# First tile stored in three column pieces, tiles 3 to 6 loaded by one DMA (contrast adjustment, 1 core)

## The chip, the core and the metric

The kernel runs on one core of one Trainium2 chip. The metric is device time in microseconds. Five runs of the kernel before gave a median of 239.35 us (239.29 to 239.66).

## What is computed

The input is a batch of 16 images with 3 channels of 512 x 512 float32 pixels. Every one of the 48 planes is moved away from its own mean and clipped:

```python
def reference(x, factor):                       # x: 16 x 3 x 512 x 512 float32, factor 1.5
    mean = np.mean(x, axis=(2, 3), keepdims=True)
    return np.clip(mean + factor * (x - mean), 0, 1).astype(np.float32)
```

The kernel computes it as `factor * x + (1 - factor) * mean`, followed by a max with 0 and a min with 1. Input and output have 50.33 MB each, and each byte crosses once.

## The kernel before

The 48 planes are cut into 12 tiles of 4 planes. A tile is 128 partitions of 8192 float32 (32 KB a partition, 4 MiB in all); 32 partitions hold one plane. `ring` is one tensor with six slots of a tile each (`BUFS = 6`); tile t lives in slot `t % 6`, is loaded there, changed in place and stored from there. Below, tiles are numbered from 0, so "tiles 3 to 6" of the title are tiles 2 to 5 in the code.

Each tile passes through `compute(t)`, in this order:

- VectorE sums columns 0 to 4351 of each partition (`tensor_reduce`, L89), and at the same time ScalarE sums the other 3840 columns by an activation with an accumulator (L92).
- TensorE multiplies both partial sums by the constant block matrix `blockw` (L94 and L95). The result, `bias[:, t]`, holds for each partition the shift of its plane.
- VectorE makes two passes over the whole tile: multiply and add (L96), then max and min (L99).
- `store` (L112) issues the tile's output DMAs from ScalarE's queue.

The order is written out by hand (`tc.manual_schedule`), and each engine works through its own list in this order. SyncE's queue issues all loads (L84): tile 0 in two parts (2048 and 6144 columns), then tiles 1 to 5, one DMA each. After `compute(t)`, the load of tile t + 6 follows; it waits until all stores of tile t have landed, since it overwrites that slot. ScalarE issues all stores, so the sum of tile t + 1 on ScalarE stands behind the stores of tile t.

The stores of tile 0 are special. `RAMP` lists eight DMAs; each takes every 4th partition from a first partition q, so 32 partitions, and a range of columns. The contiguous stretches that they write grow from 4 KB to 32 KB. All eight stand after the two whole-tile passes L96 and L99. Tiles 1 to 11 leave in one DMA each, with 128 stretches of 32 KB.

Each DMA signals its end on one of eight shared counters, so an issue can also wait for the end of an earlier DMA that had the same counter. In the program before, the sixth, seventh and eighth store of tile 0 wait in this way on ScalarE's queue, and the loads of tiles 3, 4 and 5 on SyncE's queue.

Of the kernel before, what the change touches and what calls it, by code (L numbers as in the profile page):

```python
# [1 line left out]

# [4 lines left out]


P = 128  # L10
ROW = 8192
BUFS = 6
SHORT = 2048

RAMP = [
    (0, 4, 0, 1024),
    (1, 4, 0, 2048),
    (0, 4, 1024, 4096),
    (2, 4, 0, 4096),
    (2, 4, 4096, ROW),  # L20
    (0, 4, 4096, ROW),
    (1, 4, 2048, ROW),
    (3, 4, 0, ROW),
]
SUM = 4352


@with_exitstack
def kernel(
    ctx: ExitStack,  # L30
    tc: tile.TileContext,
    x: bass.AP,
    factor: float,
    out: bass.AP,
):

    nc = tc.nc
    f32 = mybir.dt.float32  # L40
    Alu = mybir.AluOpType
    Act = mybir.ActivationFunctionType

    B, C, H, W = x.shape
    n_img, n_pix = B * C, H * W
    ppi = n_pix // ROW
    per_tile = P // ppi
    n_tiles = n_img // per_tile
    assert ppi * ROW == n_pix and per_tile * n_tiles == n_img

    factor = float(factor)
    wconst = (1.0 - factor) / float(n_pix)

    x_f = x.rearrange("b c h w -> (b c h w)")
    out_f = out.rearrange("b c h w -> (b c h w)")


    consts = ctx.enter_context(tc.tile_pool(name="consts", bufs=1))
    xpool = ctx.enter_context(tc.tile_pool(name="xpool", bufs=1))
    small = ctx.enter_context(tc.tile_pool(name="small", bufs=1))  # L60
    psum = ctx.enter_context(tc.tile_pool(name="psum", bufs=1, space=bass.MemoryType.PSUM))


    sums = small.tile([P, 2 * n_tiles], f32, name="sums")
    junk = small.tile([P, ROW - SUM], f32, name="junk")
    bias = psum.tile([P, n_tiles], f32, name="bias")

    blockw = consts.tile([P, P], f32, name="blockw")
    nc.gpsimd.memset(blockw, 0.0)  # L69
    for a in range(0, P, ppi):  # L70
        nc.gpsimd.memset(blockw[a : a + ppi, a : a + ppi], wconst)  # L71


    ring = xpool.tile([P, BUFS, ROW], f32, name="ring")

    def load(t, c0=0, c1=ROW, n=1):

        b = t % BUFS
        src = bass.AP(
            tensor=x_f.tensor,  # L80
            offset=t * P * ROW + c0,
            ap=[[ROW, P], [P * ROW, n], [1, c1 - c0]],
        )
        nc.sync.dma_start(out=ring[:, b : b + n, c0:c1], in_=src)  # L84

    def compute(t):
        xt = ring[:, t % BUFS, :]
        own = sums[:, 2 * t : 2 * t + 2]
        nc.vector.tensor_reduce(  # L89
            out=own[:, 0:1], in_=xt[:, 0:SUM], axis=mybir.AxisListType.X, op=Alu.add  # L90
        )
        nc.scalar.activation(out=junk, in_=xt[:, SUM:ROW], func=Act.Copy, accum_out=own[:, 1:2])  # L92
        shift = bias[:, t : t + 1]
        nc.tensor.matmul(shift, blockw, own[:, 1:2], start=True, stop=False)  # L94
        nc.tensor.matmul(shift, blockw, own[:, 0:1], start=False, stop=True)  # L95
        nc.vector.tensor_scalar(  # L96
            out=xt, in0=xt, scalar1=factor, scalar2=shift, op0=Alu.mult, op1=Alu.add
        )
        nc.vector.tensor_scalar(  # L99
            out=xt, in0=xt, scalar1=0.0, scalar2=1.0, op0=Alu.max, op1=Alu.min  # L100
        )
        for piece in RAMP if t == 0 else [(0, 1, 0, ROW)]:
            store(t, *piece)

    def store(t, q=0, parts=1, c0=0, c1=ROW):

        dst = bass.AP(
            tensor=out_f.tensor,
            offset=(t * P + q) * ROW + c0,
            ap=[[parts * ROW, P // parts], [1, c1 - c0]],  # L110
        )
        nc.scalar.dma_start(out=dst, in_=ring[q::parts, t % BUFS, c0:c1])  # L112

    with tc.manual_schedule():
        load(0, c1=SHORT)
        load(0, c0=SHORT)
        load(1)
        for t in range(2, BUFS):
            load(t)
        for t in range(n_tiles):  # L120
            compute(t)
            if t + BUFS < n_tiles:
                load(t + BUFS)


# [1 line left out]
_INS = ['x', 'factor']  # L127
_OUTS = [((16, 3, 512, 512), 'float32')]

_NUMBERS = {'factor': 1.5}  # L130


# [26 lines left out]
```

## Time and profile before

The profiled execution took 239.3 us, with a span of 237.5 us between its first and last instruction; the other 1.8 us lie outside of it. The clock granted to TensorE was 1.0 throughout.

| row of the profile | value |
|---|---|
| time of the profiled execution / its span | 239.3 us / 237.5 us |
| data moved | 100.67 MB, mean 424 GB/s over the span |
| VectorE busy | 162.4 us (68% of the span) |
| L89, L96, L99: one instruction on VectorE | 4.680, 4.491, 4.427 us |
| ScalarE busy | 43.2 us (18%) |
| L92: one instruction on ScalarE | 3.403 us |
| load queue (q1): packets, share of the 16 DMA engines | 1872, 49.7% |
| store queue (q10): packets, share of the 16 DMA engines | 1968, 49.1% |

The page gives for each engine the time in which it executed something. For transfers it gives what the 16 DMA engines moved, and how long the packets of each queue occupied them. A packet here is one contiguous stretch in a partition, or one 4-byte signal at the end of a DMA on one DMA engine. The page's 40 slices cut the span into equal parts of 5.94 us, and each digit is a busy share in tenths.

### The profile page before, as it was taken

The numbers are of one execution on the slowest core, as the hardware profiler recorded it, in microseconds if no ns is written. First come the engines' busy times: TensorE is split into PE (matmuls) and PEld (weight loads), VectorE is DVE, ScalarE is ACT, GpSimd is POOL, SyncE is SP. The second block draws the span as 40 slices with busy tenths as digits, with TensorE's granted clock in tenths as the row PEclk, the third lists the DMA queues.
The fourth block names the chain that finished last, engine by engine and source line by source line (L and its number), as shares of the span: only waits on it lengthen the run. The fifth ranks groups of instructions, "written<-read, shape, count | busy, mean of one in ns | idle before, by whom it ended". The sixth has DMA issues, their size and how long they took to land.

```text
span 237.5 us, 298 instructions
## 1 busy us (share of the span) xinstructions
PE 13.9 (6%) x48; PEld 11.9 (5%) x48; DVE 162.4 (68%) x36; ACT 43.2 (18%) x25; POOL 0.9 (0%) x9
## 2 busy tenths in 40 slices
PE   0010000010100101010010100101000001000000
PEld 0010000010100101010010100101000001000000
DVE  0079930059899898999989899898998658900000
ACT  2050000320505014050320505014050040000000
POOL 1000000000000000000000000000000000000000
DMA  7999999999999999999999999999999999999996
GB/s 292 414 441 441 441 410 421 367 469 430 430 414 419 436 441 441 441 441 436 441 425 430 403 425 441 441 441 441 441 436 436 425 419 415 430 441 441 441 441 265
DMA packets 3841, 100.67 MB, mean 424 GB/s; under 512 B 512, under 2 KB 512, under 8 KB 544
## 3 DMA queue, kind: packets, MB, share of 16 engines
q1 hardware_dynamic: 1872, 50.33, 49.7%
q10 hardware_dynamic: 1968, 50.33, 49.1%
q14 instruction: 1, 0.01, 0.0%
HBM read 50.33 MB, written 50.33 MB: 424 GB/s over the span
## 4 chain that ended last, share of the span: by engine, by line
DMA 42%; DVE 28%; another core or an unknown queue 8%; issue 5%; PE 2%; ACTq 1%; SPq 0%; ACT 0%; DVEq 0%
DMA out_dram<-ring 26%; DMA ring<-in_x_dram 16%; DVE ring L96 11%; DVE ring L99 11%; DVE sums L89 6%; PE bias L95 1%; ACTq L112 1%; PE bias L94 1%; SPq L84 0%; ACT junk L92 0%; DVEq L96 0%; ACTq L92 0%; DVEq L89 0%
## 5 line engine op out<-in xcount | busy, mean ns | idle before, releaser
L96 DVE TENSOR_SCALAR ring<-ring,bias 128x8192 f32<-128x8192 f32 x12 | 53.9, 4491 | 26.4 <-PE bias L95 23.4
L92 ACT ACTIVATE junk<-ring 128x3840 f32<-128x3840 f32 x12 | 40.8, 3403 | 152.5 <-DVE ring L99 86.2
L89 DVE TENSOR_REDUCE sums<-ring 128x1 f32<-128x4352 f32 x12 | 56.2, 4680 | 18.1 <-DMA ring<-in_x_dram 18.1
L99 DVE TENSOR_SCALAR ring<-ring 128x8192 f32<-128x8192 f32 x12 | 53.1, 4427 | 0.4
L94 PE MATMUL bias<-sums,blockw 128*128 128x1 f32 x24 | 7.0, 361 | 182.4 <-ACT junk L92 182.4
L94 PEld LDWEIGHTS bias<-sums,blockw 128*128 128x128 f32 x24 | 6.0, 311 | 183.3 <-ACT junk L92 167.0
L95 PE MATMUL bias<-sums,blockw 128*128 128x1 f32 x24 | 7.0, 362 | 2.0 <-DVE sums L89 1.5
L95 PEld LDWEIGHTS bias<-sums,blockw 128*128 128x128 f32 x24 | 6.1, 313 | 2.9 <-DVE sums L89 2.2
L92 ACT ACTIVATION_READ_ACCUMULATOR junk<-ring 128x1 f32 x12 | 2.2, 186 | 0.0
L92 ACT ACT_TABLE_LOAD x1 | 1.3, 1283 | 0.7 <-PEq L140 0.7
L71 POOL MEMSET blockw<- 32x32 f32 x4 | 0.5, 116 | 0.2
L69 POOL MEMSET blockw<- 128x128 f32 x1 | 0.2, 204 | 0.3 <-POOLq L140 0.3
L140 POOL MEMSET const-bfloat16-1.0<- 128x1 bf16 x1 | 0.1, 111 | 0.0
L140 POOL MEMSET const-uint8-127<- 128x1 uint8 x1 | 0.1, 111 | 0.0
L140 POOL MEMSET const-float32-1.0<- 128x1 f32 x1 | 0.1, 108 | 0.0
L140 POOL MEMSET const-float32-0.0<- 128x1 f32 x1 | 0.1, 103 | 0.2 <-issue 0.2
## 6 DMA issues: line engine op xcount, KB each, us to landing
ring<-in_x_dram SPq DMA_DIRECT2D x11, 4096.0 KB, 26.5
out_dram<-ring ACTq DMA_DIRECT2D x11, 4096.0 KB, 44.0
ring<-in_x_dram SPq DMA_DIRECT2D x1, 3072.0 KB, 11.6
out_dram<-ring ACTq DMA_DIRECT2D x3, 512.0 KB, 24.5
ring<-in_x_dram SPq DMA_DIRECT2D x1, 1024.0 KB, 4.7
out_dram<-ring ACTq DMA_DIRECT2D x1, 1024.0 KB, 24.6
out_dram<-ring ACTq DMA_DIRECT2D x1, 768.0 KB, 27.4
out_dram<-ring ACTq DMA_DIRECT2D x1, 384.0 KB, 16.3
```

Of the source, the lines that this page charges most:

```text
L69: nc.gpsimd.memset(blockw, 0.0)
L71: nc.gpsimd.memset(blockw[a : a + ppi, a : a + ppi], wconst)
L89: nc.vector.tensor_reduce(out=own[:, 0:1], in_=xt[:, 0:SUM], axis=mybir.AxisListType.X, op=Alu.add)
L92: nc.scalar.activation(out=junk, in_=xt[:, SUM:ROW], func=Act.Copy, accum_out=own[:, 1:2])
L94: nc.tensor.matmul(shift, blockw, own[:, 1:2], start=True, stop=False)
L95: nc.tensor.matmul(shift, blockw, own[:, 0:1], start=False, stop=True)
L96: nc.vector.tensor_scalar(out=xt, in0=xt, scalar1=factor, scalar2=shift, op0=Alu.mult, op1=Alu.add)
L99: nc.vector.tensor_scalar(out=xt, in0=xt, scalar1=0.0, scalar2=1.0, op0=Alu.max, op1=Alu.min)
L112: nc.scalar.dma_start(out=dst, in_=ring[q::parts, t % BUFS, c0:c1])
L140: nc = _bacc.Bacc("TRN2", target_bir_lowering=False, num_devices=1)
```

## The change

The first tile's two passes are cut by columns into three pieces of 2048, 3072 and 3072 columns (8, 12 and 12 KB a partition). Each piece is passed over twice and stored at once, by a DMA over all 128 partitions. The list `RAMP` goes. The four loads of tiles 2 to 5 become one DMA of 128 x 4 x 8192 elements, of 16 MiB; within a partition its four stretches of 32 KB come from four tiles, which lie 4 MiB apart in the input. All other loads, stores and sums stay as they are.

```diff
-RAMP = [
-    (0, 4, 0, 1024),
-    (1, 4, 0, 2048),
-    (0, 4, 1024, 4096),
-    (2, 4, 0, 4096),
-    (2, 4, 4096, ROW),
-    (0, 4, 4096, ROW),
-    (1, 4, 2048, ROW),
-    (3, 4, 0, ROW),
-]
+FIRST = (SHORT, 3072, 3072)
...
-        nc.vector.tensor_scalar(
-            out=xt, in0=xt, scalar1=factor, scalar2=shift, op0=Alu.mult, op1=Alu.add
-        )
-        nc.vector.tensor_scalar(
-            out=xt, in0=xt, scalar1=0.0, scalar2=1.0, op0=Alu.max, op1=Alu.min
-        )
-        for piece in RAMP if t == 0 else [(0, 1, 0, ROW)]:
-            store(t, *piece)
+        c = 0
+        for n in FIRST if t == 0 else [ROW]:
+            part = xt[:, c : c + n]
+            nc.vector.tensor_scalar(
+                out=part, in0=part, scalar1=factor, scalar2=shift, op0=Alu.mult, op1=Alu.add
+            )
+            nc.vector.tensor_scalar(
+                out=part, in0=part, scalar1=0.0, scalar2=1.0, op0=Alu.max, op1=Alu.min
+            )
+            store(t, c, c + n)
+            c += n
 
-    def store(t, q=0, parts=1, c0=0, c1=ROW):
-
-        dst = bass.AP(
-            tensor=out_f.tensor,
-            offset=(t * P + q) * ROW + c0,
-            ap=[[parts * ROW, P // parts], [1, c1 - c0]],
-        )
-        nc.scalar.dma_start(out=dst, in_=ring[q::parts, t % BUFS, c0:c1])
+    def store(t, c0, c1):
+        nc.scalar.dma_start(out=dram(out_f, t, c0, c1), in_=ring[:, t % BUFS, c0:c1])
 
     with tc.manual_schedule():
         load(0, c1=SHORT)
         load(0, c0=SHORT)
         load(1)
-        for t in range(2, BUFS):
-            load(t)
+        load(2, n=BUFS - 2)
```

`dram(ap, t, c0, c1)` is a new helper that names columns c0 to c1 of tile t in the input or output. The loop over the tiles is unchanged.

More of the change, by code (lines that the diff above doesn't have):

```diff
@@ L55, with dram @@
     out_f = out.rearrange("b c h w -> (b c h w)")
+    def dram(ap, t, c0=0, c1=ROW):
+        return bass.AP(tensor=ap.tensor, offset=t * P * ROW + c0, ap=[[ROW, P], [1, c1 - c0]])
     consts = ctx.enter_context(tc.tile_pool(name="consts", bufs=1))
```

## The prediction

> **What bounds the kernel now.** I read the page's 40 slices first, then the DMA queues, then the busy times by stretch, then the chain of waits around the first store, then the timeline of ScalarE's and SyncE's queues.
>
> ```profile
> DVE  0079930059899898999989899898998658900000
> DMA  7999999999999999999999999999999999999996
> ```
>
> VectorE has holes, at 30 to 48 us and at the end. The DMA row has none: 9 from the second slice to the last but one.
>
> ```profile
> q1 hardware_dynamic: 1872, 50.33, 49.7%
> q10 hardware_dynamic: 1968, 50.33, 49.1%
> ```
>
> Loads and stores together occupy the 16 DMA engines for 98.8% of the span. The bytes are fixed, so the span is data over rate, plus the start, plus the end, plus whatever is moved below the usual rate. The busy times by stretch show where that is (the last two columns are the DMA share and GB/s):
>
> ```profile
> 4.00:28.00 24.00, 1.14 (x4) 1.00 (x4) 14.37 (x4) 3.50 (x2) 0.00 (x0) 1.00 1.03 442
> 28.00:32.00 4.00, 0.00 (x0) 0.00 (x0) 3.83 (x1) 0.00 (x0) 0.00 (x0) 1.00 1.05 452
> 32.00:36.00 4.00, 0.00 (x0) 0.00 (x0) 0.00 (x0) 0.00 (x0) 0.00 (x0) 1.00 0.89 372
> 36.00:40.00 4.00, 0.00 (x0) 0.00 (x0) 0.00 (x0) 0.00 (x0) 0.00 (x0) 1.00 1.03 426
> 40.00:44.00 4.00, 0.00 (x0) 0.00 (x0) 0.00 (x0) 0.00 (x0) 0.00 (x0) 1.00 0.96 344
> 44.00:48.00 4.00, 0.00 (x0) 0.00 (x0) 0.00 (x0) 2.63 (x1) 0.00 (x0) 1.00 1.02 438
> 48.00:192.00 144.00, 11.57 (x40) 9.95 (x40) 130.62 (x29) 32.33 (x20) 0.00 (x0) 1.00 1.00 433
> ```
>
> The steady rate is 433 GB/s; 100.66 MB at it are 232.5 us, so 5.0 us of the span are start, end and slow stretches. From 28 to 48 us the mean is 406 GB/s: 20 us x (1 - 406/433) = 1.2 us lost. With 4 to 28 us, which shares packets over the window's edge, it is 44 us x (1 - 426/433) = 0.7 us. The packet records lie between: a 32 KB read takes 1.213 us everywhere else, and some 50 reads from 32.9 to 43.7 us take 1.25 to 2.0 us; their excess, over 16 engines, is 0.9 us. They follow the first three pieces of tile 0 (4, 8 and 12 KB), mostly right behind a piece's 4-byte end signals (33, 37.5 and 42.3 us). Behind the 16 to 32 KB pieces none is stretched.
>
> How the two queues share the engines is in the queue rows of 31 to 44 us and of 72 to 192 us:
>
> ```profile
> q1 hardware_dynamic: 148, 4.26, 83.2%
> q10 hardware_dynamic: 145, 0.84, 15.4%
> ...
> q10 hardware_dynamic: 899, 26.31, 50.8%
> q1 hardware_dynamic: 881, 25.59, 49.4%
> ```
>
> Packets go one for one, whatever their size: with short store packets the loads get most of the time, with equal packets half. The chain shows what held tile 1:
>
> ```profile
> 28.49 16.33 DMA out_dram<-ring
> 44.83 0.02 issue
> 44.85 0.48 ACTq L112
> 45.32 0.05 issue
> 45.37 0.07 ACT junk L92
> ```
>
> ScalarE sat until 44.85 us before its eighth store issue, so the sum of tile 1 began at 45.37, and store 1 was issued at 59.02. Nothing of that stopped the DMA row.
>
> **The change, part by part.**
>
> *Packets.* For tile 0's stores each engine gets 24 packets (8 of 8 KB, 16 of 12 KB) in place of 16. By the records a packet takes 0.159, 0.309, 0.460, 0.611, 1.213 us for 4, 8, 12, 16, 32 KB: 0.008 us beside the bytes. So +8 x 0.008 = +0.07 us. DMAs fall from 32 to 24, each with one end signal of 0.009 us an engine: -0.07 us. Sum 0.
>
> *VectorE in tile 0.* L96 and L99 (4.49 + 4.43 us) become six instructions. No row has these widths; proportional they cost the same 8.92 us, and the nearest row for an instruction's fixed part is POOL's 0.10 to 0.20 us, so 4 x 0.2 = +0.8 us at most that I expect, hidden as the DMA engines read on. The first piece is done at 18.28 + 2.2 to 2.6 = about 20.8 us (now 27.25), the last at about 28.1.
>
> *ScalarE.* Three issues instead of eight; none waits for a transfer that is still running. The sum of tile 1 starts behind the third, at 28.5 instead of 45.4 us, and by the rows of tile 0 (3.6 + 1.2 + 8.95 us) store 1 is issued near 42.4 instead of 59.0.
>
> *The one load.* It removes three issues of 0.33 us on SyncE and two waits there (29.3 us for a load to land); SyncE bounds nothing. But tiles 2 to 5 now land together, and VectorE waits. When? Loads 0 and 1 are in by 2.2 + 8.39 MB/433 = 21.6 us. Now the first store packets come after 30 us (the queue rows of 27 to 30 us have none) for an issue at 27.27; with the same 4 us, the pieces flow from about 25 us. Until then the load passes 2.8 of its 32 packets an engine. Then 24 rounds, 24 x 1.213 + 8 x 0.309 + 16 x 0.460 = 39.0 us, to 64.0; then 5.2 rounds against store 1, 5.2 x 2.43 = 12.6, to 76.6. It lands near 77 us; bounds are 2.2 + 25.2 MB/433 = 60.3 (no store passes) and 2.2 + 33.6 MB/433 = 79.7 (both stores first).
>
> *What is late next.* Tile 2 starts on VectorE at 77 instead of 58.9. A tile takes 14.3 us there (start to start in the timeline of tiles 2 and 3), so tile 2 is ready at 91.4, tile 3 at 105.7, tile 11 at 77 + 143 = 220 (now 207.3). Do the DMA engines run dry? Before store 3, they have loads 0 to 7 and stores 0 to 2: 11 x 4.194 = 46.1 MB, until 2.2 + 106.5 = 108.7 us. Store 3's data flows at 105.7 + 0.4 issue + 1.0 (0.74 to 1.75 us, the first load's packets) = 107.1: 1.6 us to spare. Before store 2: 41.9 MB, until 99.1 against 92.8. Before store 4: 13 tiles, until 128 against 121.4. Before store 11: 96.5 MB, until 225 against 221.4. The tightest place has cover, so the late tiles cost 0. If the load lands at its upper bound, store 3 flows at about 110.2 and the gap is 1.5 us; cover ends at a landing past 78.6. Load 6 waits for three ends instead of eight; store 0 ends by about 65 to 70 (load 6 now starts at 69.6), behind the large load in the queue anyway: 0.
>
> *The stretched reads.* What becomes of the 0.9 us is open. Lower bound 0: -0.9. Upper bound, by rounds: six rounds of 4 to 12 KB lost 0.9, 0.15 each, so 24 would lose 3.6: +2.7. I take the row it is nearest to: the excess sits at three end signals of short pieces, and the new kernel has three. So 0.9 again, net 0.
>
> *A rule against it.* In the stretch from 48 to 192 us, where an engine's successive reads are neighbouring rows of 32 KB, the rate is 433 GB/s; no row here has reads 4 MiB apart. The Trainium skill (DMA: Bandwidth & Descriptors, Latency and other measured facts) reports that a partition pitch of 4 MiB halves a copy's rate, from 207 to 103 GB/s a direction. [...]
>
> Sum on the profiled execution: 239.3 + 0.07 - 0.07 + 0 = 239.3; the median is 239.35, the same within the runs. A difference below 0.2% (0.48 us) can't be told from none here.
>
> **Rivals.**
>
> *Faster: the stretch goes.* If it belongs to the 32-partition pieces or the 4 KB start, the reads keep 1.213 us: 239.35 - 0.9 = 238.45. For: pieces from 16 KB up stretch nothing. Against: two of the three new pieces have the 12 KB of the worst stretched moment. 0.28.
>
> *Slower: every short round stretches.* All 24 rounds with 8 and 12 KB packets lose 0.15 us: 239.35 + 2.7 = 242.05. It decides from (0.9 + 0.48)/24 = 0.06 us a round. For: the lowest rate, 344 GB/s, is with 12 KB pieces. Against: the excess lies at few moments, not at every round. 0.18.
>
> *Slower: the DMA engines run dry near 108 us.* Landing past 78.6 us opens a gap of up to 1.5 us: up to 240.9. Against: the one-for-one sharing puts it at 77. 0.12.
>
> *Not what it says:* the load split again, or the ring not free. The built program has one 128 x 4 x 8192 transfer; this is in the forecast's rest.
>
> **How the numbers follow.** Forecast "same" 0.42, at 239.3. Faster 0.28, slower 0.18 + 0.12 = 0.30. The range goes from below the faster case (238.3) past the gap case (240.9) to 241.2; it leaves out the 24-round case, 0.18.
>
> **What would show it.** DMA row without a hole; the first store issue near 21 us, store 1 near 42; VectorE idle from about 42 to 77, then without pause for ten tiles; the last load landed near 190; store 11 issued near 220. A DMA share well below 1 around 97 to 110 us would show the gap; a rate below 420 GB/s through 25 to 65 us the stretched rounds; 433 through 25 to 65 the faster case. I am wrong if the last store is issued after 225 us or the large load lands past 80.

## The result and the profile after

| | kernel before | kernel after |
|---|---|---|
| median time | 239.32 us (46 runs, 239.04 to 240.42) | 239.96 us (27 runs, 239.38 to 241.23) |
| median span | 237.5 us (237.3 to 237.8) | 238.0 us (237.4 to 239.1) |
| median time outside of the span | 1.79 us (1.74 to 1.85) | 2.06 us (1.78 to 2.18) |

The span and the outside time of the kernel before come from 69 further runs of it, timed beside the experiments.

The change made the kernel slower by 0.64 us: the ratio is 1.0027, with an interval of 1.002 to 1.0033. About 0.5 us of the loss lies inside the span and 0.25 to 0.3 us outside of it; medians do not add up exactly. The forecast was "same" at 239.3 us. The time lies inside the range, but 0.27% is more than the 0.2% that counted as no change. The profiled execution of after took 239.85 us, with a span of 237.7 us, so its trace holds only about 0.2 us of the 0.5 us.

The 40 slices of after, VectorE and the DMA engines:

```profile
DVE  0079989000001899898989989899898989989000
DMA  7999999999999999999999999999999999999996
```

VectorE's hole is longer and starts later than before (41.6 to 71.3 us in whole slices), and VectorE works until later: three idle slices at the end, where before had five. The DMA row has no hole, as before. The two queues (packets, MB, share of the 16 DMA engines) and the one large load (KB, then us from issue to landing):

```profile
q1 hardware_dynamic: 1824, 50.33, 49.6%
q10 hardware_dynamic: 2016, 50.33, 49.1%
...
ring<-in_x_dram SPq DMA_DIRECT2D x1, 16384.0 KB, 74.2
```

It landed 74.2 us after its issue at 2.1 us, so at about 76.3 us, where 77 was predicted. The waits of VectorE for a load (total us, number of waits, longest) and ScalarE's timeline (start, duration, engine, line, operation, count) give the rest of the schedule:

```profile
DVE sums L81 <- DMA ring<-in_x_dram: 47.1, 2, 34.3
```

```profile
20.75 7.39 ACTq L101 DMA_DIRECT2D out_dram<-ring  x3
...
42.10 0.34 ACTq L101 DMA_DIRECT2D out_dram<-ring  x1
76.42 3.40 ACT L84 ACTIVATE junk<-ring 128x3840 f32<-128x3840 f32 x1 [44.68 <-DMA ring<-in_x_dram]
...
90.78 0.34 ACTq L101 DMA_DIRECT2D out_dram<-ring  x1
...
105.08 0.34 ACTq L101 DMA_DIRECT2D out_dram<-ring  x1
```

The first piece leaves at 20.75 us, store 1 is issued at 42.10 us, and then VectorE waits for 34.3 us. Tile 2 starts at 76.4 us, store 2 is issued at 90.78 us, store 3 at 105.08 us, store 11 at 219.4 us. The prediction had 20.8, 42.4, 77, 91.4, 105.7 and 220. So the schedule is the predicted one within 0.7 us. What was not foreseen stands in the busy times by stretch (the last two columns are the DMA share and GB/s):

```profile
24.00:64.00 40.00, 1.17 (x4) 1.00 (x4) 17.25 (x6) 3.50 (x2) 0.00 (x0) 1.00 1.00 426
64.00:88.00 24.00, 1.17 (x4) 1.00 (x4) 10.85 (x3) 3.50 (x2) 0.00 (x0) 1.00 1.01 437
92.00:96.00 4.00, 1.18 (x4) 1.00 (x4) 3.35 (x1) 2.67 (x2) 0.00 (x0) 1.00 0.93 393
```

From 92 to 96 us the rate is 393 GB/s; the kernel before had 434 GB/s in that stretch. The DMA queues between 88.5 and 93.5 us show what surrounds it, first in after, then in before:

```profile
q1 hardware_dynamic: 80, 2.10, 98.0%
```

```profile
q10 hardware_dynamic: 35, 1.15, 53.1%
q1 hardware_dynamic: 33, 0.98, 45.5%
```

After has no row for q10 there: nothing is stored. Store 1's last data packet ends at 85.8 us and its last end signal at 87 us; store 2 is issued at 90.78 us, and its first packet comes 4.2 us later, at 94.95 us. Reads alone keep the engines at 98.0%, so no hole shows in the DMA row. In the packet records six reads from 90.7 to 94.1 us, on five of the 16 DMA engines, take 0.15 to 0.47 us longer than the 1.213 us of a 32 KB packet.

Sorted by engine, the packet records of these two executions also give the end of each of the 16. The mean end of the transfers is even earlier than before, 235.78 against 235.98 us. The slowest engine, with which the span ends, finishes at 236.53 us against 236.33 us. It lags the mean by 0.75 us, and 0.64 us of its time are the two reads of these six that fell to it.

### The profile page after: what moved, and what is told of

The parts are those of the page before. It is cut to its first block, busy times and chain, and to the rows that moved or that the text cites. A ratio compares the mean times of both kernels' runs of the same rounds, so it can differ in the third digit from the quotient of the medians.

```text
span 237.7 us, 286 instructions
## 1 busy us (share of the span) xinstructions
PE 14.0 (6%) x48; PEld 12.0 (5%) x48; DVE 162.9 (69%) x40; ACT 43.2 (18%) x25; POOL 0.9 (0%) x9
## 3 DMA queue, kind: packets, MB, share of 16 engines
q1 hardware_dynamic: 1824, 50.33, 49.6%
q10 hardware_dynamic: 2016, 50.33, 49.1%
## 5 line engine op out<-in xcount | busy, mean ns | idle before, releaser
L91 DVE TENSOR_SCALAR ring<-ring,bias 128x8192 f32<-128x8192 f32 (+2 forms) x14 | 54.3, 3882 | 8.9 <-PE bias L87 4.4
L94 DVE TENSOR_SCALAR ring<-ring 128x8192 f32<-128x8192 f32 (+2 forms) x14 | 53.4, 3817 | 0.5
## 6 DMA issues: line engine op xcount, KB each, us to landing
ring<-in_x_dram SPq DMA_DIRECT2D x1, 16384.0 KB, 74.2
```

Source lines behind the costliest of these rows:

```text
L91: nc.vector.tensor_scalar(out=part, in0=part, scalar1=factor, scalar2=shift, op0=Alu.mult, op1=Alu.add)
L94: nc.vector.tensor_scalar(out=part, in0=part, scalar1=0.0, scalar2=1.0, op0=Alu.max, op1=Alu.min)
```

## The experiments

Each was timed beside the kernel before, with 5 to 12 runs. The ratio is to that kernel, with its 95% interval.

| label | time, us | ratio | median span, us | outside, us |
|---|---|---|---|---|
| after | 239.96 | 1.0027 [1.002, 1.0033] | 238.0 | 2.06 |
| e1_pieces_only | 241.59 | 1.0106 [1.009, 1.0121] | 239.6 | 1.99 |
| e2_merge_only | 240.52 | 1.0056 [1.0042, 1.007] | 238.6 | 1.95 |
| e3_two_pairs | 239.44 | 1.0007 [0.9998, 1.0015] | 237.3 | 2.07 |
| e4_whole_first | 240.34 | 1.0043 [1.0031, 1.0055] | 237.9 | 2.43 |
| e5_merge_act_pad | 239.87 | 1.0032 [1.002, 1.0044] | 237.9 | 1.98 |
| e6_pairs_hold | 239.82 | 1.0021 [1.001, 1.0033] | 237.75 | 2.05 |
| e7_before_hold | 240.85 | 1.0066 [1.0046, 1.0086] | 238.9 | 1.95 |
| e8_pairs_act_pad | 239.66 | 1.0016 [1.0007, 1.0025] | 237.6 | 2.06 |
| e9_before_nohold | 239.40 | 1.0009 [1.0, 1.0017] | 237.5 | 1.91 |
| e10_three_and_one | 239.50 | 1.0011 [1.0002, 1.0019] | 237.4 | 2.08 |
| e11_pieces_gated | 241.18 | 1.0076 [1.0052, 1.0099] | 239.15 | 2.03 |
| e12_two_tiles_in_pieces | 239.24 | 0.9997 [0.9989, 1.0006] | 237.3 | 1.95 |

**The two parts of the change, alone.** First the pieces with the four single loads of before:

```diff
-        load(2, n=BUFS - 2)
+        for t in range(2, BUFS):
+            load(t)
```

> The three column pieces as in the changed kernel, but tiles 2 to 5 loaded by four DMAs as before. Store-gap theory (the large load lands four tiles at once, the store queue is empty from 87 to 95 us, and reads beside the restarting store are stretched on some engines): the stores never stop here, so no stretched read after 90 us, and the time is that of before, 239.1 to 239.5 us (ratio 0.999 to 1.001). Short-pieces theory (24 short store packets an engine cost the time, wherever the loads stand): as slow as the changed kernel, 239.8 to 240.2 us (ratio 1.002 to 1.0035).

It took 241.59 us, the slowest of all, and neither theory had that. Then the one load alone. The stores of tile 0 are nearly those of before: the two entries of RAMP that begin with partition 2 became one, which stands behind two others, so tile 0 leaves in seven DMAs instead of eight:

```diff
-    (2, 4, 0, 4096),
-    (2, 4, 4096, ROW),
     (0, 4, 4096, ROW),
     (1, 4, 2048, ROW),
+    (2, 4, 0, ROW),
...
-        for t in range(2, BUFS):
-            load(t)
+        load(2, n=BUFS - 2)
```

> Tiles 2 to 5 loaded by one DMA, tile 0 stored by every-4th-partition DMAs as before, but seven of them (the third group of partitions leaves whole, as the last), since an eighth would wait on ScalarE's queue for the large load by a shared counter. Store-gap theory: VectorE gets tile 2 near 76 us, the store queue runs empty until about 92 us, some reads after 85 us are stretched, time as in the changed kernel, 239.7 to 240.3 us (ratio 1.002 to 1.0035). Short-pieces theory: time as before, 239.1 to 239.5 us.

It took 240.52 us. Store 2 is issued at 91.02 us, and the store queue is empty from 82 to 94.5 us, longer than in after. One engine ends at 237.80 us, most at 235.7 to 236.0 us. The time is above the range of the store-gap theory, and the trace (of the slowest of six runs) does not bear out its mechanism: eight reads from 94.2 to 96.8 us are stretched by 0.03 to 0.28 us, none of them on the slowest engine. That one falls behind later, by reads stretched by 0.52 us at 125.2 us and 0.28 us at 145.1 us and by 0.4 us of idle time at 167.2 us. The two parts do not add up: alone they cost 2.3 and 1.2 us (the latter with the other stores of tile 0), together 0.64 us. So the pieces cost the most, but only beside the single loads.

**The late store 2, taken away.** After, with two loads of two tiles each:

```diff
-        load(2, n=BUFS - 2)
+        load(2, n=2)
+        load(4, n=2)
```

> The changed kernel with two loads of two tiles (2 and 3, then 4 and 5) in place of one load of four. Store-gap theory: the first pair lands near 50 us, tile 2 is stored near 65 us while store 1 still flows, so the store queue never empties, no stretched read after 90 us, 239.1 to 239.5 us. Short-pieces theory: 239.8 to 240.2 us. If the 4 MiB stride itself costs something, it stays slow by about half of the difference.

It took 239.44 us, and the span is that of before. Store 2 is issued at 62.1 us. The DMA queues of 88.5 to 93.5 us now hold both:

```profile
q1 hardware_dynamic: 32, 1.05, 48.5%
q10 hardware_dynamic: 32, 1.05, 48.5%
```

After 90 us three reads are stretched, by less than 0.09 us each. What is left to before, 0.0007, lies outside of the span. A load of three tiles and a single one keep more of the large load and bring store 2 forward as well, to 74.88 us:

```diff
-        load(2, n=BUFS - 2)
+        load(2, n=BUFS - 3)
+        load(BUFS - 1)
```

> The changed kernel with one load of tiles 2 to 4 (12 MiB) and one of tile 5. The large load should land near 63 to 66 us, tile 2 be stored near 80 us, before store 1 ends (85 us), so the stores never stop. Late-store theory: no stretched read after 85 us, span 237.2 to 237.7, about 239.4 us (with 2.05 us outside of the span). Theory that large loads or 4 MiB steps cost: between the pairs and the changed kernel or above, 239.6 to 240.2 us.

It took 239.50 us with a span of 237.4 us. The sign named for it did not come, though: six engines have reads stretched by 0.12 to 0.49 us from 85.5 to 87.9 us, where store 2 follows store 1 within 0.9 us. That is 0.14 us an engine on average, against 0.12 us at the restart in after. So a stretched read is not proper to an empty store queue. A third way keeps the one load of four tiles and fills the time before store 2 with more pieces, by storing tile 1 in three pieces too:

```diff
-        for n in FIRST if t == 0 else [ROW]:
+        for n in FIRST if t < 2 else [ROW]:
```

> The changed kernel with tile 1 cut into the same three pieces as tile 0. Short packets give the large load a bigger share, so it lands near 73 us and store 2 is issued near 88 us; store 1, in 24 short packets an engine, lasts to about 91 us, so the stores never stop although four tiles still come by one load. Late-store theory: no stretch at 90 to 95 us, span 237.2 to 237.7, 239.2 to 239.6 us. Theory that the large load or the pieces cost: 239.9 to 240.6 us.

The median is 239.24 us and the span 237.3 us: the loss is gone with the large load in place. The store pieces have short packets, so the loads get more of the engines; the large load lands near 72.4 us and store 2 is issued at 87.18 us, while store 1's last packets flow until 90.6 us. The stores never stop:

```profile
q10 hardware_dynamic: 125, 2.32, 108.0%
```

This is the stretch in which after had q1 alone. Now the loads are missing: none runs from 84.7 to 95.1 us. After has such a silence of the loads too, from 107.1 to 114.8 us; by e12's median it costs nothing. The profiled execution of e12 was the slowest of its eleven, though (240.00 us, span 238.0 us). In it, at the restart of the loads, one store packet takes 0.63 us longer at 95.3 us, and this engine ends at 236.65 us, 0.8 us behind the next. E12 is the quickest variant here, but its interval does not set it apart from before.

**The late store 2, put in without the rest.** In e3, and in the kernel before, a copy of one column on VectorE holds tile 2 until tile 5 has landed:

```diff
+        if t == 2:
+            nc.vector.tensor_copy(out=gate, in_=ring[:, 5, 0:1])
```

> The kernel with two loads of two tiles (239.44 us), with one 128x1 copy on VectorE ahead of tile 2's sum, which reads a column of tile 5 and so holds tile 2 until the second pair has landed, near 77 us. The loads are those of the pairs, the stores stand as in the changed kernel (none from about 87 to 95 us). Late-store theory (the empty store queue and its restart beside running reads put single DMA engines behind): span 237.7 to 238.3, time 239.8 to 240.3 us. Theory that the 16 MiB load itself costs (its order, its 4 MiB steps): as the pairs without the hold, 239.3 to 239.6 us.

It took 239.82 us, 0.38 us over e3. The two medians are not clearly apart: five of e6's twelve runs are as short as e3's. The spans reach from 237.2 to 238.5 us, and the profiled execution was one of the short ones (237.3 us), although its store queue is empty from 88.5 to 93.5 us too. An empty store queue therefore does not cost the same in every execution.

> The kernel before with the same 128x1 copy ahead of tile 2's sum, so that tile 2 is held until tile 5 has landed, near 76 us, and store 2 is issued near 91 instead of 73 us. Late-store theory: a gap in the stores from about 88 to 95 us and a span longer by 0.3 to 0.8 us, 239.6 to 240.1 us, with the RAMP and the single loads untouched. Theory that the 16 MiB load or the pieces cost: 239.1 to 239.5 us, as before.

The same hold in the kernel before made it 240.85 us, more than that theory had. For its control the copy reads tile 2 itself, and so holds nothing:

```diff
-            nc.vector.tensor_copy(out=gate, in_=ring[:, 5, 0:1])
+            nc.vector.tensor_copy(out=gate, in_=ring[:, 2, 0:1])
```

> The control of the kernel before with the hold: the same 128x1 copy on VectorE, but reading a column of tile 2 itself, so it holds nothing back. Late-store theory: the copy is free, stores as before (store 2 issued near 73 us), span 237.3 to 237.8, 239.1 to 239.5 us. If the added instruction itself made the kernel with the hold slow: 240.3 to 241.3 us. The time outside of the span (1.78 us before, 1.95 with the hold) shows whether a change of the program alone moves it.

That is 239.40 us, with a span of 237.5 us. So the hold costs 1.4 us of span in a kernel that has no part of the change. ScalarE's timeline shows when store 2 is issued, in e7 and then in e9:

```profile
91.25 0.34 ACTq L115 DMA_DIRECT2D out_dram<-ring  x1
```

```profile
73.46 0.34 ACTq L115 DMA_DIRECT2D out_dram<-ring  x1
```

The DMA queues from 88.5 to 93.5 us in e7 and then in e9:

```profile
q1 hardware_dynamic: 80, 2.10, 99.1%
```

```profile
q10 hardware_dynamic: 38, 1.21, 56.1%
q1 hardware_dynamic: 33, 0.92, 42.5%
```

And the busy times from 92 to 96 us, e7 and then e9 (rate at the end):

```profile
92.00:96.00 4.00, 0.72 (x3) 0.64 (x3) 3.81 (x1) 3.13 (x2) 0.00 (x0) 1.00 0.96 352
```

```profile
92.00:96.00 4.00, 0.92 (x4) 0.75 (x4) 3.25 (x2) 0.00 (x0) 0.00 (x0) 1.00 1.01 434
```

E7 repeats after's picture, and more strongly. Reads run alone from about 88 to 95.9 us, and the read in flight right before the first store packet, at 94.2 to 94.8 us, takes 0.33 to 0.59 us longer on all 16 engines. The engines then end at 236.3 to 237.2 us, on average 0.58 us later than before.

**The time outside of the span.** The packet records show instruction fetches of 8 KB each. In before one stands inside the span, at 197.2 us; in after it stands behind the last instruction, at 239.6 us. A theory was that this later fetch is ScalarE's and costs the time. A pad of 48 activations of one column was to move it, in after and in e3:

```diff
+        if 2 <= t < 8:
+            for _ in range(8):
+                nc.scalar.activation(out=spare, in_=blockw[:, 0:1], func=Act.Copy)
```

> The changed kernel with 48 one-column activations added on ScalarE in tiles 2 to 7, where it waits 10 us a tile anyway (they write a spare column; nothing else changes). Code-fetch theory (part of the loss lies outside of the span: 2.0 to 2.15 us there instead of 1.76, because a shorter ScalarE program fetches its last 8 KB of code behind the end instead of at 197 us, as before): the time outside of the span goes back to 1.7 to 1.8 us, the span stays 237.4 to 238.3, the time falls by 0.25 us to about 239.7. If the fetch costs nothing: time and outside part as in the changed kernel, 239.96 and 2.0 us.

> The kernel with two loads of two tiles (239.44 us, span 237.3 in most runs, 2.1 us outside), with the same 48 one-column activations on ScalarE. Code-fetch theory: 1.75 us outside of the span, so 239.1 us, level with before or a little under it (ratio 0.998 to 1.000). If the fetch costs nothing: 239.4 us.

Times outside of the span are 1.98 us (after: 2.06) and 2.06 us (e3: 2.07), so almost nothing came back. But the pad did not do what it was meant to: a fetch now stands inside the span, at 139.8 us in e5 and 112.6 us in e8, and another still stands behind the last instruction, at 239.7 and 239.8 us. E7 and e9 tell more. They have no fetch behind the end, and still 1.95 and 1.91 us outside, so a late fetch is not the whole of it. Whether it is a part is open.

E8 is also 0.2 us slower than e3, with 0.3 us more span, although its stores never stop. In its trace ten engines have reads stretched by 0.09 to 0.57 us from 103.7 to 106.2 us, at the change from store 2 to store 3. Why the pad brings that is open.

**The pieces beside single loads.** Two runs went for the cause of e1's loss. Without pieces, tile 0 is stored whole:

```diff
-FIRST = (SHORT, 3072, 3072)
+FIRST = (ROW,)
```

> No pieces at all: tile 0 leaves in one DMA of 128 x 32 KB after two whole passes, tiles 2 to 5 in four loads. Store-gap theory: the stores never stop, so not slower than before; the excess of the reads from 20 to 90 us (0.9 us an engine before, 0.7 in the changed kernel) is that of one store's start, below 0.4 us, so 238.7 to 239.3 us (ratio 0.997 to 1.000). Short-pieces theory: the fastest of the four, 238.4 to 238.9 us, with no stretched read from 28 to 90 us.

This is e1 with that edit. It took 240.34 us, where both theories had it no slower than before. Here the stretched reads are early: 1.23 us an engine, all in reads that begin from 29.0 to 32.7 us, around the first store packet at 32.5 us. Its engines end close together, at 235.95 to 236.37 us, and it has the longest time outside of the span, 2.43 us. So about 0.4 us of its loss lie inside the span and 0.65 us outside. The other run is e1 with the loads of tiles 4 and 5 held back, so that fewer loads queue up at the start:

```diff
         for t in range(2, BUFS):
+            if t > 3:
+                nc.gpsimd.tensor_copy(out=ring[:, t, 0:1], in_=ring[:, t - 2, 0:1])
             load(t)
```

> Pieces with single loads again (241.59 us), but the load of tile 4 is issued only after tile 2 has landed and that of tile 5 after tile 3 (a one-column GpSimd copy into the slot, overwritten by the load, holds it back), so that the load queue is as short as in the kernel before. Theory of the deep load queue (four loads issued within 22 us put engines out of step): 239.1 to 239.7 us. Theory that the short pieces beside single loads do it: 241 to 242 us, as without the gates.

It took 241.18 us, within the noise of e1, so the depth of the load queue is not the cause. What the trace of e1 does show is the end. In the DMA row from 234 to 238 us, cut into slices of 0.1 us, a digit marks slices in which packets begin; a 32 KB packet ends 1.2 us later. Before, then after, then e1:

```profile
DMA  0000099797770000000000000000000000000000
```

```profile
DMA  0779999907000700000000000000000000000000
```

```profile
DMA  0000999007777000000007070000000000000000
```

Before, the last packets begin within 0.7 us. After has most of them earlier, and a single one at 235.3 us, later than any of before. In e1 two packets begin at 236.1 and 236.3 us, nearly a microsecond behind the other 14 engines. By the records, four engines are out of step in e1. At the changes from one store to the next, every 19.5 us or so from 82 to 180 us, the two slowest get a stretched read (up to 0.5 us) and the two others a stretched store packet (about 0.1 us). In e11 two engines end behind the others, at 236.8 and 237.7 us, with such packets too. Why the pieces put engines out of step beside single loads, and not beside merged ones, is open.

## Why the prediction was wrong

**Packets, VectorE, ScalarE, the one load: right.** The queues have 2016 and 1824 packets; the wider pieces take 1.82 and 1.76 us, 0.10 to 0.14 us over proportional, within the 0.2 us allowed; the issues and the landing came within 0.7 us. The 1.213 us of a packet and the one-for-one sharing of before's rows carried the landing of a load that did not exist yet.

**The stretched reads: slightly mis-sized, in after's favour.** From 20 to 90 us they cost 0.69 us an engine, where 0.9 was kept (0.94 in before's records). The rate of 426 GB/s from 24 to 64 us lies between the signs named for the short rounds and for the faster case. The 8 and 12 KB rounds did not stretch as such. Neither that rival nor the faster one came. The 0.25 us gained on average goes with the earlier mean end, and it did not reach the time.

**The rule that spoke against the change.** The large load's four stretches in a partition lie 4 MiB apart, and from 24 to 64 us, while it ran, the rate was 426 GB/s. The halving that the Trainium skill (DMA: Bandwidth & Descriptors, Latency and other measured facts) reports is for a pitch of 4 MiB from partition to partition; here neighbouring partitions stay 32 KB apart. No such loss appears here, and e12 keeps the load at no loss.

**What is late next: this step failed.** It counted the bytes that were ready for all DMA engines together, and concluded that the late tiles cost 0 as long as the engines do not run dry. They did not: the share from 88.5 to 93.5 us was 98.0%. But the cover was made of loads only. The text worked out that store 2's data flows at 92.8 us and that store 1 was the last before it; it never asked when store 1 ends, 87 us, and what the engines do when a store queue that was empty starts again. It also gave store 2 only 1.4 us from the issue to its data, where 4.2 us passed, so the silence grew to 9 us (85.8 to 94.95 us). There are two errors in the step. First, not only a dry engine costs: a silent store queue and its restart beside running loads cost span too, 1.4 us in e7 and about 0.5 us in after. Second, it worked with the mean of 16 engines, and the span ends with the slowest: in the traced executions after's mean end gained 0.20 us and its slowest engine lost 0.20 us.

That a late store 2 costs span is shown in the old kernel, by e7 against its control e9 (+1.4 us). In the new one e3, e10 and e12 take the silence out in three ways, each with about before's span. E12 does so with store 2 issued only 3.6 us earlier than in after, which points to the silence of the stores and not to the late tiles as such. E6 against e3 (+0.45 us of span) points the same way, but it is weak: its runs overlap with e3's, and e8, without any silence, lies 0.3 us above e3. The rival of the dry engines named the place near 108 us and a landing past 78.6 us; the load landed at 76.3 us, and the loss lay one store earlier.

How the silence costs the time is shown in e7 alone, where the stretched reads at the restart (0.6 us an engine) match the later mean end. In after it is argued: the six stretched reads lie there, and two of them on the slowest engine, but e10 has as much stretch at an ordinary change of stores without the loss, and e2's slowest engine falls behind later. E6's short execution shows that the cost varies.

**The constant outside of the span: the second step that failed.** The sum took 1.8 us from before's execution. All changed programs lie between 1.91 and 2.43 us, even e9, which only adds one instruction (1.91). A third to four tenths of after's loss are here. A late instruction fetch is not the whole of it, since e7 and e9 have none; what it is stays open.

## What to carry to other kernels

In a kernel that the DMA engines bound, look not only for holes in the DMA row but also for stretches in which one of the two queues is missing: list the queues by stretch, and count a silence of the stores beside running loads as a cost, here about 0.5 us (after) to 1.4 us (e7). Merging loads makes the first of the merged tiles as late as the last; two loads of two, three and one, or more stores queued ahead of the gap kept the span. Where a change is worth less than 1 us, work with the slowest DMA engine and with the time outside of the span, not with the mean and the span alone.

## What was not expected of the hardware

- A read in flight when a silent store queue starts again was stretched from 1.213 us by 0.33 to 0.59 us on all 16 engines in e7. In after, reads from the issue to the restart were stretched by 0.15 to 0.47 us on five engines. A change from one store to the next within 0.9 us did the same to six engines in e10 (0.12 to 0.49 us).
- A silent load queue can do it too: at its restart in e12's slowest run one store packet was stretched by 0.63 us.
- The 16 DMA engines end apart, within 0.4 us in e4 and by 1.9 us in e1, and the engines that are out of step in e1 get stretched packets again at later changes of store.
- The time outside of the span follows the program: 1.79 us before, 1.91 us with one VectorE instruction more, 2.43 us in e4.
